# Ten weight splits by two transfers and scalar's negative, in the stage of the local attention

## The chip, the cores and the metric

The kernel runs on one core of a Trainium2 chip. The core has a matrix engine (TensorE, PE in the profile, with PEld for its weight loads), three engines for elementwise work (VectorE or DVE, ScalarE or ACT, GpSimd or POOL), a queue that only issues transfers (SyncE or SP), and 16 DMA engines that all queues share. Each engine works through its own queue strictly in order; a semaphore makes one wait for another. The metric is the device time of one execution in microseconds (us).

## The reference

One decoder layer on 512 tokens of width 1024, in float32. A shared normalised input h is multiplied by one wide matrix; its columns are split up for a recurrent branch, a local attention and their gates:

```python
h = rmsnorm(x, norm_mix_g[i])
proj = h @ w_in[i]
qk_ml, v_ml, o_ml, if_pre, q_sw, k_sw, v_sw, g_a, g_b = jnp.split(proj, split_idx, axis=-1)
qk_ml = jax.nn.silu(causal_depthwise_conv(qk_ml, conv_qk[i]))
...   # h_ml: chunkwise mLSTM of qk_ml, v_ml and gates, then y_a
y_b = swa_with_sinks(q_sw, k_sw, v_sw, sinks[i])   # 16 query heads, 4 key heads, window 128
merged = sigmoid(g_a) * (y_a @ w_branch_a[i]) + sigmoid(g_b) * (y_b @ w_branch_b[i])
x = x + merged @ w_out[i]
...   # squared-ReLU MLP of width 4096, a gated per-layer embedding, a last RMSNorm
```

What bears on the change: q_sw (1024 columns) and qk_ml (1024 columns) are each computed as eight projections of 128 columns, `w_qsw` and `w_qkml` in the kernel.

## The kernel before, in words

**Matmuls in three products.** TensorE multiplies in a rounded format (float32r). To keep float32's precision every operand is held as two tiles: a rounded part and the remainder that rounding left. A product is then three matmuls: rounded by rounded, rounded by remainder, remainder by rounded (`pairs`, `chain`, line 171). A projection (`proj_T`, `mm_T`) has 8 slices of the inner dimension, so 24 matmuls of 128x128 by 128x512.

**How a weight is split.** `load_w` takes a raw tile `wr` (128 x 1024 float32, 512 KB, four buffers) that a transfer from SP fills (`load_raw`, line 152). Then `split` makes the two parts: ACT casts it into `wh` (line 137), and DVE subtracts `wh` from `wr` into `wl` (line 138). `wh` and `wl` have four buffers each (`WB = 4`), shared by every weight of the kernel, so a weight can be split as soon as the weight four places earlier has been read by its last matmul.

**A split by transfer exists already.** `split_by_transfer` (lines 143 to 147) is used for eight sums of the activations: ACT casts the sum into the rounded part, ACT writes the sum's rounded negative into the second tile, and a transfer from POOL's queue adds the sum to that.

**The stage of the local attention.** Sixteen units of attention (`swa_probs`, `swa_out`; scores on PE at lines 689 and 690, copies and predicated copies at 700 and 701, exponentials on ACT at 712, the normalising product on DVE at 716, transposes at 726, the product with the values at 747, the split of the result into `yb` at 137 and 138) depend on long chains between PE, ACT and DVE. To keep PE at work beside them, eleven projections are put between the units as `fill`: `qk_proj(0)`, `q_proj(4)` to `q_proj(7)`, then `qk_proj` of 4, 1, 5, 2, 6 and 3. `qk_proj(7)` follows the loop. `q_proj` evicts its bank with a cast on ACT (424) and a subtraction on DVE (425); `qk_proj` with a scaled copy on ACT (666) and three multiply-adds on DVE (668), the convolution. Ahead of the stage stand the projections of the gates and `q_proj` 1 to 3; behind it the sigmoids of `silu` and the recurrent branch, with the eight projections of `w_b` between its steps.

**What sets the order.** The program's order gives priorities; when the program is built, a list scheduler walks through it with its own durations, and at each moment puts on every engine the ready instruction of highest priority. The result is one fixed order for each queue. Only the waits on semaphores are left for run time. So a change of one instruction can give other queues another order, too.

The parts that the change touches:

Of the kernel before, what the change touches and what calls it, by code (L numbers as in the profile page):

```python
# [11 lines left out]
F32R = mybir.dt.float32r  # L12
AF = mybir.ActivationFunctionType
ALU = mybir.AluOpType
AX = mybir.AxisListType

P = 128
# [3 lines left out]
KT = D // P  # L21
# [8 lines left out]
WB = 4  # L30
# [6 lines left out]
def block_kernel(  # L37
# [29 lines left out]
    nc = tc.nc  # L67
    V, A, G, T = nc.vector, nc.scalar, nc.gpsimd, nc.tensor


    def pool(stack, name, **kw):
        return stack.enter_context(tc.tile_pool(name=name, bufs=1, reuse_waits="tile", **kw))
# [4 lines left out]
    wp = pool(ctx, "wp")  # L77
# [9 lines left out]
    def nm(s):  # L87
        n_names[0] += 1
        return f"{s}_{n_names[0]}"


    def ps_g():
        return pp.tile([P, 512], F32, tag="g", bufs=2, name=nm("psg"))
# [12 lines left out]
    def act_f(n="f"):  # L106
        return ap.tile([P, 512], F32, tag="act", bufs=NACT, name=nm(n))

    def act_r(n="r"):
        return ap.tile([P, 512], F32R, tag="act", bufs=NACT, name=nm(n))  # L110
# [4 lines left out]
    def big_hl(n):  # L115

        hl = [bp.tile([P, KT, 512], F32R, tag="big", bufs=2, name=nm(n)) for _ in range(2)]
        return hl, [[t[:, k, :] for t in hl] for k in range(KT)]

    def tk(n):  # L120
        return tp_.tile([P, NH * (DV + 1)], F32, tag="tk", bufs=4, name=nm(n))
# [7 lines left out]
    def r32(t):  # L129
        return t.bitcast(F32)  # L130
# [3 lines left out]
    def split(dst, src, scale=None):  # L134

        if scale is None:
            A.copy(dst[0], src)  # L137
            last_low[0] = V.tensor_sub(dst[1], src, r32(dst[0]))  # L138
        else:
            A.activation(dst[0], src, AF.Copy, scale=scale)  # L140
            V.scalar_tensor_tensor(dst[1], src, scale, r32(dst[0]), ALU.mult, ALU.subtract)
# [8 lines left out]
    def load_raw(src, n):  # L150
        raw = wp.tile([P, 1024], F32, tag="wr", bufs=WRB, name=nm("wr"))
        nc.sync.dma_start(out=raw[:, :n], in_=src)
        return raw

    def load_w(src, n, dims, raw=None):

        if raw is None:
            raw = load_raw(src, n)
        parts = [wp.tile([P, 1024], F32R, tag=t, bufs=WB, name=nm(t))[:, :n] for t in ("wh", "wl")]
        split(parts, raw[:, :n])  # L160
        return [q.rearrange("p (k c) -> p k c", k=dims) for q in parts]

    def pairs(a, b):

        return [(a[0], b[0]), (a[0], b[1]), (a[1], b[0])]
# [3 lines left out]
    def chain(ps, ops, first, last, parts=False):  # L169
        for i, (l, r) in enumerate(ops):  # L170
            last_mm[0] = T.matmul(ps, l, r, start=first and i == 0, stop=last and i == len(ops) - 1, skip_group_check=parts)  # L171
# [13 lines left out]
    def mm_T(ps, w, acts, first=True, last=True):  # L185

        ops = []
        for k in range(len(acts)):
            ops += pairs([q[:, k, :] for q in w], acts[k])
        chain(ps, ops, first, last)  # L190
# [99 lines left out]
    h2, hT = big_hl("h")  # L290
# [49 lines left out]
    for m in range(NT):  # L340
# [7 lines left out]
        ps = ps_g()  # L348
        for c in range(3):
            mm_tok(ps[:, :264], wv[c], hT[K3[c]], m, first=c == 0, last=c == 2)  # L350
        t = sp.tile([P, 256], F32, tag="vs", bufs=4, name=nm("vs"))
# [1 line left out]
        gate_in = V.tensor_add(gt[:, m, :], ps[:, 256:264], bif)  # L353
        vs.append(t)

    def proj_T(wd, i, bank=ps_g):
        ps = bank()
        mm_T(ps, load_w(wd[i], KT * P, KT), hT)
        return ps

    dp = pool(ctx, "dp", space=bass.MemoryType.DRAM)
# [3 lines left out]
    with tc.issue_after(gate_in.ins):  # L365
        hi, lo = [r32(t[:, :, :P]) for t in h2]
# [37 lines left out]
    for i in range(2):  # L404
        ps = proj_T(w_ksw, i, ps_t)
        both = [act_r("kk"), act_r("kk")]
        low = [act_r("kl"), act_r("kl")]
        for ab in range(2):
            s, o = HALF[ab], HALF[1 - ab]
            A.copy(both[ab][s, :], ps[s, :])  # L410
            V.tensor_sub(low[ab][s, :], ps[s, :], r32(both[ab][s, :]))
            nc.sync.dma_start(out=r32(both[ab])[o, :], in_=r32(both[ab])[s, :])
            nc.sync.dma_start(out=r32(low[ab])[o, :], in_=r32(low[ab])[s, :])
        kk.append(both)
        kl.append(low)

    qs = {}

    def q_proj(i):
        ps = proj_T(w_qsw, i)  # L420
        for ab in range(2):
            s, o = HALF[ab], HALF[1 - ab]
            t = act_r("qs")
            A.copy(t[s, :], ps[s, :])
            V.tensor_sub(t[o, :], ps[s, :], r32(t[s, :]))
            qs[i, ab] = t

    q_proj(0)

    S3, S4 = [], []  # L430
# [48 lines left out]
    for m in range(NT):  # L479
        t = tk("vm").rearrange("p (h d) -> p h d", h=NH)  # L480
# [3 lines left out]
    def by_tokens(w, post, own_first=False):  # L484

        raws = quads(w, ["wr", "wr", "lm", "lm", "wr", "wr", "lm", "lm"])
        b = ps_a()
        X, Y, Z = [ps_t(), ps_t()], [b[:, :512], b[:, 512:]], [ps_g(), ps_g()]

        def prod(ps, f, w, kh, first, last=False):  # L490
            for t in range(2):
                ops = []
                for k in range(2):
                    ops += pairs([h[:, t * P : (t + 1) * P] for h in f[2 * kh + k]], [h[:, k, :] for h in w])
                chain(ps[t], ops, first and kh == 0, last and kh == 1, True)

        seven(lambda r: load_w(None, 1024, 2, r), prod, X, Y, Z, [raws[2 * i : 2 * i + 2] for i in range(4)], post, own_first)
# [70 lines left out]
    with tc.issue_after(last_mm[0].ins):  # L568
        for t in range(NT):
            for s in range(t + 1):  # L570
                c = (t * NT + s) * 4
                T.transpose(pgc[:, c : c + 4], gg[t][:, s * P : (s + 1) * P], ident[:4, :4])
            c = (NT * NT + t) * 4
# [22 lines left out]
    def gate_proj(wd):  # L596

        out_d = [None] * 4
        for j in range(2):
# [21 lines left out]
            def post(what, ps):  # L621
# [7 lines left out]
                else:  # L629
# [6 lines left out]
                    A.activation(o, ps, AF.Sigmoid)  # L636

            seven(lambda r: load_w(None, 1024, 4, r), prod, X, Y, Z, [raws[i : i + 1] for i in range(4)], post)
            for nh in range(2):
                d = dp.tile([P, 2, 512], F32, name=nm("gd"))  # L640
# [16 lines left out]
    for i in range(1, 4):  # L657
        q_proj(i)
# [1 line left out]

    qk = [None] * 8

    def qk_proj(i):
        ps = proj_T(w_qkml, i)
        acc = act_f("acc")
        A.activation(acc, ps, AF.Copy, scale=cw[:, i * 4 + 3 : i * 4 + 4])
        for s in range(1, 4):
            V.scalar_tensor_tensor(
                acc[:, s:], ps[:, : S - s], cw[:, i * 4 + 3 - s : i * 4 + 4 - s], acc[:, s:], ALU.mult, ALU.add
            )  # L670
        qk[i] = acc
# [86 lines left out]
    for n in (3, 2, 1):  # L758
        V.tensor_sub(vd[n], vs[n], vs[n - 1])

    fill = [lambda: qk_proj(0)] + [lambda i=i: q_proj(i) for i in range(4, 8)]
    fill += [lambda i=i: qk_proj(i) for i in (4, 1, 5, 2, 6, 3)]
    for u in range(LOOK):
        swa_probs(*units[u])
    for u in range(16):
# [4 lines left out]
        if u % 2:  # L770
            swa_out(*units[u][:2])

    qk_proj(7)

    for h in range(NH):
# [551 lines left out]
    for m in range(NT):  # L1327
        for o, n in ((0, 512),) if m == 0 else ((0, 256), (256, 256)):
            ps = ps_g()[:, :n]
# [108 lines left out]
```

## Time and profile before

| | |
|---|---|
| median of 3 runs | 880.56 us (880.06 to 881.1) |
| profiled execution | 879.82 us |
| its span, first to last instruction | 878.0 us |
| mean granted TensorE clock | 0.998 |
| PE busy | 866.8 us (99%) |
| DVE busy | 657.2 us (75%) |
| ACT busy | 483.5 us (55%) |
| POOL busy | 34.1 us (4%) |
| HBM read and written | 91.30 MB and 8.40 MB |

The profile is one execution. Its views: the page's totals; groups of instructions (line, engine, operation, out<-in by the program's names, count | busy us, mean ns | idle time ahead of them and who ended it); waits (who waited for whom: us, times, longest); the chain of waits that ended last, followed back from the end (start, us, what); timelines (start, us, instruction, idle ahead of it); and busy time by stage. Matmuls are pipelined and their ends are modelled, so one is drawn longer than the distance to the next. A line such as L137 can be a helper's, so the tile names tell more.

### The profile page before, as it was taken

How to read it: one execution, taken by the hardware profiler on the slowest of the kernel's cores; microseconds unless marked ns; L12 is line 12 of the kernel's file. 1: busy time of each engine (PE TensorE's matmuls, PEld its weight loads, DVE VectorE, ACT ScalarE, POOL GpSimd, SP SyncE). 2: the span in 40 equal slices, each digit the busy share in tenths (PEclk: the TensorE clock that was granted, in tenths of full speed). 3: DMA queues.
4: the chain of work that ended last, by engine and by line, in shares of the span. 5: the costliest groups of instructions: out<-in, count | busy, mean ns of one | idle time of the engine just before them, and what ended most of it. 6: DMA issues, size and time to landing. Idle time of an engine off the chain costs nothing.

```text
span 878.0 us, 11545 instructions
## 1 busy us (share of the span) xinstructions
PE 866.8 (99%) x4372; PEld 725.6 (83%) x4372; DVE 657.2 (75%) x966; ACT 483.5 (55%) x803; POOL 34.1 (4%) x58
## 2 busy tenths in 40 slices
PE   8999999999999999999999999999999999999996
PEld 7888889998777777788888888888888888888886
DVE  6999887875789876665896669756956794698557
ACT  6684554544676768743344665356435634564843
POOL 1111010000000000000020000000000000020000
PEclk9999999999999999999999999999999999999999
DMA  7765244435122162274244612530352054125302
GB/s 266 211 180 186 73 150 169 165 111 196 52 73 72 49 199 88 97 240 144 72 75 145 236 49 71 197 106 10 124 185 75 1 186 149 49 52 141 121 0 96
DMA packets 32793, 106.74 MB, mean 122 GB/s; under 512 B 4573, under 2 KB 4573, under 8 KB 32738
## 3 DMA queue, kind: packets, MB, share of 16 engines
q1 hardware_dynamic: 27570, 93.15, 31.2%
q0 software_dynamic: 5024, 12.59, 5.9%
q8 instruction: 34, 0.56, 0.3%
q10 hardware_dynamic: 144, 0.26, 0.1%
q14 instruction: 21, 0.17, 0.1%
HBM read 91.30 MB, written 8.40 MB: 114 GB/s over the span
## 4 chain that ended last, share of the span: by engine, by line
PE 90%; DVE 4%; ACT 3%; DMA 2%; issue 1%; SPq 0%; ACTq 0%; DVEq 0%
PE psg L171 50%; PE psp L171 23%; PE psa L171 7%; PE pst L171 4%; PE psa L831 1%; PE pst L747 1%; DVE wl L138 1%; DMA wr<-in_w_vsif 1%; ACT lm L712 1%; PE psa L819 1%; PE psa L689 1%; PE psa L690 1%; ACT wh L137 0%; DMA wr<-in_w_gb 0%; PE psp L980 0%
## 5 line engine op out<-in xcount | busy, mean ns | idle before, releaser
L137 ACT CAST wh<-wr 128x1024 fp32r<-128x1024 f32 x138 | 144.8, 1051 | 180.3 <-PE psg L171 74.8
L138 DVE TENSOR_TENSOR wl<-wr,wh 128x1024 fp32r<-128x1024 f32 x138 | 167.8, 1219 | 85.9 <-ACT wh L137 84.6
L171 PE MATMUL psg<-x,wh 128*128 128x512 f32 x512 | 157.7, 389 | 0.0
L171 PE MATMUL psp<-wh,uf 128*128 128x512 f32 x448 | 138.6, 389 | 0.0
L171 PEld LDWEIGHTS psg<-x,wh 128*128 128x128 f32 x512 | 96.0, 188 | 19.9
L171 PE MATMUL psg<-x,wl 128*128 128x512 f32 x256 | 99.6, 389 | 0.0
L171 PEld LDWEIGHTS psp<-wh,uf 128*128 128x128 f32 x448 | 84.1, 188 | 17.5
L171 PE MATMUL psp<-wl,uf 128*128 128x512 f32 x224 | 87.2, 389 | 0.0
L171 PE MATMUL psg<-h,wh 128*128 128x512 f32 x256 | 81.1, 395 | 0.7 <-DVE rc L715 0.7
L137 ACT CAST wh<-wd 128x1024 fp32r<-128x1024 f32 x44 | 46.2, 1052 | 54.0 <-PE psp L171 21.9
L138 DVE TENSOR_TENSOR wl<-wd,wh 128x1024 fp32r<-128x1024 f32 x44 | 53.1, 1217 | 14.7 <-ACT wh L137 14.5
L171 PEld LDWEIGHTS psg<-x,wl 128*128 128x128 f32 x256 | 48.0, 188 | 10.0
L171 PEld LDWEIGHTS psg<-h,wh 128*128 128x128 f32 x256 | 47.0, 188 | 11.2 <-issue 1.6
L171 PE MATMUL psg<-h,wl 128*128 128x512 f32 x128 | 50.5, 395 | 0.0
L138 DVE TENSOR_TENSOR uf<-F,uf 128x1792 fp32r<-128x1792 f32 (+2 forms) x20 | 33.0, 1652 | 21.8 <-ACT uf L137 21.8
L171 PEld LDWEIGHTS psp<-wl,uf 128*128 128x128 f32 x224 | 42.0, 188 | 8.7
L171 PE MATMUL psg<-yb,wh 128*128 128x512 f32 x128 | 41.3, 402 | 0.1
L171 PE MATMUL psg<-ya,wh 128*128 128x512 f32 x128 | 39.5, 390 | 0.0
L137 ACT CAST uf<-F 128x1792 fp32r<-128x1792 f32 (+2 forms) x20 | 27.9, 1396 | 20.5 <-DVE F L1133 20.4
L1157 DVE SCALAR_TENSOR_TENSOR xk<-psp,r,xk 128x512 f32<-128x512 f32 x48 | 33.7, 744 | 5.5 <-PE psp L171 5.2
L171 PE MATMUL psg<-hS,wh 128*128 128x256 f32 x192 | 35.6, 284 | 0.0
L171 PE MATMUL psa<-h,wh 128*128 128x256 f32 x192 | 35.3, 285 | 0.2 <-ACT p L625 0.2
(322 smaller groups left out, 1745.6 us busy)
## 6 DMA issues: line engine op xcount, KB each, us to landing
wr<-in_w_up SPq DMA_DIRECT2D x32, 512.0 KB, 3.3
wd<-in_w_down SPq DMA_DIRECT2D x24, 512.0 KB, 3.7
wr<-in_w_qsw SPq DMA_DIRECT2D x8, 512.0 KB, 4.3
gd<-gr POOLq DMA_DIRECT2D x8, 512.0 KB, 3.7
wr<-in_w_qkml SPq DMA_DIRECT2D x8, 512.0 KB, 3.2
wr<-in_w_b SPq DMA_DIRECT2D x8, 512.0 KB, 3.2
gl<-gd SPq DMA_DIRECT2D x8, 512.0 KB, 3.4
wr<-in_w_a SPq DMA_DIRECT2D x8, 512.0 KB, 4.4
```

The costliest lines, as they stand in the source:

```text
L137: A.copy(dst[0], src)
L138: last_low[0] = V.tensor_sub(dst[1], src, r32(dst[0]))
L171: last_mm[0] = T.matmul(ps, l, r, start=first and i == 0, stop=last and i == len(ops) - 1, skip_group_check=parts)
L689: T.matmul(o, q[:, n * P : (n + 1) * P], kk[kp][ab][:, k0 : k0 + 256], start=True, stop=False)
L690: T.matmul(o, q[:, n * P : (n + 1) * P], kl[kp][ab][:, k0 : k0 + 256], start=False, stop=True)
L712: A.activation(lm3[:, g, :], lm3[:, g, :], AF.Exp, bias=nmx[:, g : g + 1], scale=0.125, accum_out=sm[:, g : g + 1])
L747: T.matmul(o[HALF[ab], :], v[:, c : c + 64], w[:, ab * 512 : (ab + 1) * 512], start=j == 0, stop=j == len(terms) - 1)
L819: T.matmul(psc, qk[4 + h][:, n0 : n0 + P], qk[h][:, n0:], start=True, stop=True, skip_group_check=True)
L831: last_mm[0] = T.matmul(pn[:, t % 2, : DV + 1], wT[s][:, t * P : (t + 1) * P], vm[s][:, h, :], start=s == 0, stop=s == t, skip_group_check ...
L1157: V.scalar_tensor_tensor(o, ps[:, t, :], r2[:, 2 * toks + t : 2 * toks + t + 1], o, ALU.mult, ALU.add)
```

## The change

For the ten projections `q_proj(4)` to `q_proj(7)` and `qk_proj` of 4, 1, 5, 2, 6 and 3, the weight is no longer loaded raw by SP and split by ACT and DVE. A transfer from POOL's queue reads it from memory and casts it into `wh` on the way. ACT then writes the negative of `wh` into `wl`. A second transfer from POOL's queue reads the weight once more and adds it to `wl`, which leaves the remainder. The raw tile and DVE's subtraction go, ACT's cast becomes ACT's negative, and two transfers stand in place of one. `qk_proj(0)`, `qk_proj(7)` and every other weight stay as they were.

```diff
+    def load_by_dma(src, n, dims):
+        hi, lo = [wp.tile([P, 1024], F32R, tag=t, bufs=WB, name=nm(t))[:, :n] for t in ("wh", "wl")]
+        nc.gpsimd.dma_start(out=hi, in_=src)
+        A.activation(lo, r32(hi), AF.Copy, scale=-1.0)
+        nc.gpsimd.dma_start(out=lo, in_=src, accum_op=ALU.add)
+        return [q.rearrange("p (k c) -> p k c", k=dims) for q in (hi, lo)]
+
-    def load_w(src, n, dims, raw=None):
-
+    def load_w(src, n, dims, raw=None, by_dma=False):
+
+        if by_dma:
+            return load_by_dma(src, n, dims)
...
-    def proj_T(wd, i, bank=ps_g):
+    def proj_T(wd, i, bank=ps_g, by_dma=False):
         ps = bank()
-        mm_T(ps, load_w(wd[i], KT * P, KT), hT)
+        mm_T(ps, load_w(wd[i], KT * P, KT, by_dma=by_dma), hT)
...
-    fill = [lambda: qk_proj(0)] + [lambda i=i: q_proj(i) for i in range(4, 8)]
-    fill += [lambda i=i: qk_proj(i) for i in (4, 1, 5, 2, 6, 3)]
+    fill = [lambda: qk_proj(0)] + [lambda i=i: q_proj(i, True) for i in range(4, 8)]
+    fill += [lambda i=i: qk_proj(i, True) for i in (4, 1, 5, 2, 6, 3)]
```

`q_proj` and `qk_proj` take `by_dma=False` as well and hand it to `proj_T`.

More of the change, by code (lines that the diff above doesn't have):

```diff
@@ L417, in block_kernel, with q_proj @@
     qs = {}
-    def q_proj(i):
-        ps = proj_T(w_qsw, i)
+    def q_proj(i, by_dma=False):
+        ps = proj_T(w_qsw, i, by_dma=by_dma)
         for ab in range(2):
@@ L661, in block_kernel, with qk_proj @@
     qk = [None] * 8
-    def qk_proj(i):
-        ps = proj_T(w_qkml, i)
+    def qk_proj(i, by_dma=False):
+        ps = proj_T(w_qkml, i, by_dma=by_dma)
         acc = act_f("acc")
```

## The prediction

> **What bounds the kernel now.** I read the page first, for the engines' totals.
>
> ```profile
> PE 866.8 (99%) x4372; PEld 725.6 (83%) x4372; DVE 657.2 (75%) x966; ACT 483.5 (55%) x803; POOL 34.1 (4%) x58
> ```
>
> PE (TensorE) is busy for 866.8 of 878.0 us and the change takes no matmul away, so nothing that it does to another engine shows unless PE waits for that engine. The second view is the busy time by stage, for the stage that the change touches (from the first fill projection to the end of the local attention) and the one behind it.
>
> ```profile
> core 0: us, PE busy (x) PEld busy (x) DVE busy (x) ACT busy (x) POOL busy (x), PEclk, DMA share, GB/s
> 203.00:325.00 122.00, 120.72 (x616) 92.75 (x615) 94.11 (x199) 76.25 (x231) 0.88 (x2) 1.00 0.29 95
> 325.00:350.00 25.00, 24.87 (x108) 19.55 (x107) 18.38 (x36) 22.55 (x55) 0.00 (x0) 1.00 0.37 128
> ```
>
> In 122.00 us PE shows 1.28 us of idle time. DVE (VectorE) has 94.11 us of work there, ACT (ScalarE) 76.25, POOL (GpSimd) 0.88; the DMA engines are used to 0.29. So DVE is the busiest helper, but PE is the bound, and the gain can't be DVE's saving: it is at most what PE waits. The third view, the waits of PE in that window, names them all.
>
> ```profile
> PE psg L171 <- DVE rc L715: 0.7, 1, 0.7
> PE psa L689 <- DVE lm L701: 0.5, 1, 0.5
> PE pst L747 <- ACT pT L728: 0.2, 1, 0.2
> ```
>
> Idle time understates a wait, because each matmul is drawn longer than its pitch. The chain of waits gives the pitch (24 matmuls in 5.46 us, 0.2275 each; q1 to q3 run 72 of them without a gap) and the timeline of PE gives the starts around the two larger waits.
>
> ```profile
> 203.85 16.35 PE psg L171 x72
> 309.43 5.46 PE psg L171 x24
> ...
> 235.15 1.03 PE L726 MATMUL psa<-ident,lm 128*128 128x128 f32 x8
> 235.94 0.71 PE L171 MATMUL psg<-h,wh 128*128 128x512 f32 x2
> ...
> 263.00 0.39 PE L171 MATMUL psg<-h,wh 128*128 128x512 f32 x1
> 263.86 0.39 PE L689 MATMUL psa<-kk,qs 128*128 128x256 f32 x1 [0.47 <-DVE lm L701]
> ...
> 297.17 1.03 PE L726 MATMUL psa<-ident,lm 128*128 128x128 f32 x8
> 298.85 0.70 PE L171 MATMUL psg<-h,wh 128*128 128x512 f32 x2 [0.65 <-DVE rc L715]
> ```
>
> From 263.00 to 263.86 is 0.86 where 0.23 would do: a loss of 0.63. Eight transposes take 0.79 undisturbed (235.15 to 235.94) but 1.68 at 297.17: a loss of 0.89. These two are 1.52 us. Two smaller places remain:
>
> ```profile
> 239.03 0.39 PE L171 MATMUL psg<-h,wh 128*128 128x512 f32 x1
> 239.57 0.65 PE L747 MATMUL pst<-pT,vs 128*64 128x512 f32 x2 [0.16 <-ACT pT L728]
> ...
> 329.81 0.40 PE L171 MATMUL psg<-yb,wl 128*128 128x512 f32 x1
> 330.35 0.50 PE L171 MATMUL psg<-yb,wh 128*128 128x512 f32 x1
> ```
>
> Each is 0.54 where 0.23 would do, 0.31 lost, 0.62 together. So all that PE loses to others from 203 to 350 us is 2.14 us. That is the ceiling of this change.
>
> **The change part by part.** *DVE loses ten subtractions.* The groups of the window:
>
> ```profile
> L138 DVE TENSOR_TENSOR wl<-wr,wh 128x1024 fp32r<-128x1024 f32 x16 | 19.5, 1220 | 10.4 <-ACT wh L137 9.5 <-PE psg L171 0.8
> L137 ACT CAST wh<-wr 128x1024 fp32r<-128x1024 f32 x15 | 15.7, 1050 | 10.6 <-issue 6.8 <-PE psg L171 3.6 <-ACT yb L137 0.2
> ```
>
> Ten times 1.22 is 12.2 us of DVE's 94.11, and none of it is on PE's path by itself. Where it stands on the path is seen in the chain of waits ahead of the two larger losses:
>
> ```profile
> 242.61 0.16 ACT yb L137
> ...
> 254.42 1.23 DVE wl L138
> ...
> 296.41 0.69 ACT acc L666
> 297.22 0.17 DVE sm L713
> 297.39 1.31 DVE acc L668 x2
> ```
>
> The first loss, at 263.86, ends a chain that holds only DVE and ACT work from 242.61 us on, and the subtraction at 254.42 is a link of it. Without its 1.23 us the scores' matmul is free earlier by more than the 0.63 lost, so I count the 0.63 in full. The second loss is less sure: PE waits for a bank that DVE reads in L668, and these reads stand behind a sum (L713) that waits for ACT, which itself waits for PE until 296.41 (L666). The subtraction that goes, just before, shortens DVE's queue, but if the order of L713 and L668 stays, the 0.89 stays. I count half, 0.45. Sum: 1.08, say 1.1 us.
>
> *ACT trades ten casts for ten negatives.* No negative of 128x1024 stands in the trace. The rows of the sums that are split by transfer already have both kinds at half the size:
>
> ```profile
> L145 ACT CAST hS<-s x8: 603/607/622, 33.4 to 53.5; 128x512 fp32r<-128x512 f32 x8
> L146 ACT ACTIVATE hS<-s x8: 627/628/633, 33.9 to 54.0; 128x512 fp32r<-128x512 f32 x8
> L147 POOL DMA_DIRECT2D hS<-s x8: 837/852/1003, 34.8 to 54.9; - x8
> DMA to landing us min/median/max: 3.2/4.4/6.7
> ```
>
> 0.02 us more for 512 columns, so 0.02 to 0.04 each and at most 0.4 us over ten, on an engine with 45.75 us idle in the window: nothing, unless the place of the negative is bad (a rival below). It has a new wait, for the casting transfer, and behind it in ACT's queue stand the exponentials of the attention (L712), for which DVE and then PE wait.
>
> *POOL gets twenty transfers, SP loses ten.* An issue costs 0.53 us (a 512 KB store from POOL) to 0.85 (L147), so 10.6 to 17 us over ten weights on a queue that is empty: between its last store and the next transfer POOL has nothing.
>
> ```profile
> 205.69 0.53 POOL L641 DMA_DIRECT2D gd<-gr  x1 [2.35 <-ACT gr L636]
> 449.24 5.21 POOL L1033 DMA_DIRECT2D xk<-q  x6 [243.01 <-ACT q L1028]
> ...
> gd<-gr POOLq DMA_DIRECT2D x8, 512.0 KB, 3.7
> wr<-in_w_qkml SPq DMA_DIRECT2D x8, 512.0 KB, 3.2
> ```
>
> ```profile
> L152 SPq DMA_DIRECT2D wr<-in_w_qkml x8: 327/328/328, 194.6 to 255.7; - x8
> ```
>
> SP saves ten issues at 0.33 us, which nobody waits for; the loads of w_b behind them no longer wait for a free raw buffer and go out earlier, into the first casting transfers. The weights are read twice, 5 MB more in a stage where the DMA share is 0.29.
>
> *The new round trip.* A weight's two buffers come free when the projection four places earlier has read them, exactly as now. Then: issue, casting transfer, negative, issue, adding transfer, matmul. The tightest is the first (q4): its buffer is q1's, and q1 to q3 follow one another without attention work between them.
>
> ```profile
> 221.47 0.63 PE L171 MATMUL psg<-h,wh 128*128 128x512 f32 x2
> 325.23 0.63 PE L171 MATMUL psg<-yb,wh 128*128 128x512 f32 x2
> ...
> 209.18 1.05 ACT L137 CAST wh<-wr 128x1024 fp32r<-128x1024 f32 x1 [3.78 <-issue]
> ...
> 228.73 0.63 PE L171 MATMUL psg<-h,wh 128*128 128x512 f32 x2
> ```
>
> The first two rows are the first matmul of the twelve projections from qk0 to qk7 and the first one behind them. The cast shows when the buffer was free, the matmul when the weight is needed: 19.55 us of lead. No casting transfer is in the trace; the nearest rows are 3.7 us (the POOL store of the same size) and 3.2 (the SP load). I take 3.7, with ends at 3.2 and 7.4, twice that. The adding transfer has 256 KB in 4.4 us; for 512 KB the ends are 4.4 and 8.8, and I take the middle, 6.6. The trip is 0.85 + 3.7 + 1.05 + 0.85 + 6.6 = 13.05, at the far ends 0.85 + 7.4 + 1.05 + 0.85 + 8.8 = 18.95, and some wait in ACT's queue on top. POOL's own rhythm (issue, landing, negative, issue) is 0.85 + 3.7 + 1.05 + 0.85 = 6.45 us per weight, below the 8.6 us at which the stage uses them on average (221.47 to 325.23 for twelve projections). So PE does not wait for the transfers: cost 0, and if the cover were gone, the trip's excess over 19.55, once.
>
> Does DVE's work hold up POOL's issues? The eight issues of L147 took 0.837 to 1.003 us, with DVE at work beside them. The Trainium skill, "SBUF — State Buffer", section "Who interferes with whom", speaks against moving loads to this queue: GpSimd and VectorE share a port pair, and a VectorE copy, cast or tensor-scalar in a two-port mode locks out GpSimd, which then can't write descriptors. The groups of DVE in this window hold no copy, cast or tensor-scalar, so by that rule too the issues stay short and the sum is the same; were one blocked behind a DVE instruction, the trip would be about 1.2 us longer, inside the lead, and only the late negative below would become likelier.
>
> **Sum.** The profiled execution took 879.82 us, 1.82 over its span and 0.74 under the median of 880.56. 879.82 - 1.1 = 878.7 for such a run, and against the median 880.56 - 1.1 = 879.5. That is 0.12%, below the 0.2% that I treat as the least a measurement of this kernel can tell from no change.
>
> **The rivals.** *All of PE's waits go.* The order of the queues is drawn anew at build time, with a DVE that is 12.2 us lighter; if no loss of the 2.14 us is left and none is new, 878.4, faster by 0.24%. For it: every loss but the last lies in this window, and DVE is the busiest helper. Against: two of the four end on ACT's work, which doesn't shrink.
>
> *Nothing goes.* The 0.89 and the small ones hang on ACT, and new waits take the place of the 0.63: 880.6.
>
> *The negative comes too early in ACT's queue* (slower). The order is fixed at build time by a guess of when the casting transfer lands; if it lands later by d, ACT stands at the negative for d and the attention's exponentials behind it are late by d. DVE's freed 1.22 us make up for that much, so it decides from d = 1.2 on. Landings of 512 KB differ by more than this between queues and times:
>
> ```profile
> DMA to landing us min/median/max: 3.0/3.3/7.4
> ```
>
> (the raw loads of all the weights, by line). With d = 2 at all ten, 7.8 us; about half of the ten lie where the chain is DVE and ACT work and PE has no lead, so 3.9: 884.5. For it: the chain from 242.61 to 263.86 has no slack at all. Against: ACT is idle for 45.75 of 122 us, mostly waiting for others, and the landing of most loads is close to 3.3.
>
> *The adding transfer is late for PE* (slower). At the far ends and behind 3 us in ACT's queue the first trip is 22 us, 2.4 over the lead, and PE waits 2.4 at 228.73: 880.56 - 1.1 + 2.4 = 881.9; if it holds for the second weight too, 884.3. Against: the middle of the estimates leaves 6 us.
>
> **How the numbers follow.** The forecast has 0.33; nothing goes 0.11; all waits go 0.18; the late negative 0.30; the late adding transfer 0.08. Faster is the third, 0.18; within 0.2% the first two, 0.44; slower the last two, 0.38. The likeliest case's own range is 878.8 to 880.6 (both larger losses gone, or none). The range over all runs from 878.3 (the ceiling) to 884.6 (the priced late negative and the late second transfer); what is left out is a worse late negative.
>
> **What would show it.** Right: POOL with some 15 us more work from 209 us on, DVE's work in the stage near 82 us, ten L138 rows of wl fewer, no PE wait for L701 near 263, casting transfers that land in about 4 us, adding ones in 5 to 9. The late negative: ACT's waits led by a DMA into wh, and exponentials behind it; PE's waits on scores or transposes over 3 us. The late transfer: a PE wait on a DMA into wl at the first of the ten. I am wrong if PE's busy total moves (its work is the same), or if the stage changes by more than 2.1 us downwards.

## The result, and the profile after

The changed kernel takes 885.55 us (median of five, 885.26 to 886.13) against 880.17 us before: ratio 1.0061, 95% interval 1.0048 to 1.0074. It is slower by 5.4 us. The forecast was 879.5, with a range up to 884.6; the direction of the likeliest case was wrong, and the time lies outside the range.

The page's totals after (lines of the changed file stand ten below those of before from L171 on, so `chain` is L181 and the scores L699 and L700):

```profile
PE 869.2 (98%) x4372; PEld 727.3 (82%) x4372; DVE 647.1 (73%) x956; ACT 484.5 (55%) x803; POOL 48.1 (5%) x78
```

DVE lost ten instructions and 10.1 us (12.2 were worked out), POOL gained twenty and 14.0 us (10.6 to 17). PE's own total, which was not to move, rose by 2.4 us, of which the slow clock shown below makes about 1.7. The busy time by stage says where the loss is (start and end, busy us of PE, PEld, DVE, ACT and POOL, granted clock, DMA share):

```profile
203.00:220.00 17.00, 17.00 (x81) 14.21 (x80) 5.10 (x7) 4.96 (x7) 3.03 (x5) 1.00 0.69 199
220.00:240.00 20.00, 17.86 (x90) 15.00 (x88) 9.45 (x21) 10.76 (x28) 3.08 (x5) 0.91 0.53 127
240.00:265.00 25.00, 23.14 (x113) 17.07 (x114) 18.18 (x46) 18.70 (x60) 4.20 (x7) 1.00 0.56 127
```

PE is idle for 2.14 us of the stretch from 220 to 240 us, and of the whole stage in that stretch alone its granted clock is below 1.00, at 0.91. PE's waits after and ACT's longest ones:

```profile
PE psa L699 <- DVE qs L435: 2.0, 1, 2.0
...
PE pst L757 <- ACT pT L738: 0.9, 2, 0.6
PE psa L736 <- DVE lm L711: 0.8, 1, 0.8
PE psa L699 <- DVE lm L711: 0.7, 1, 0.7
PE psg L181 <- DVE acc L678: 0.5, 1, 0.5
...
ACT wl L159 <- DMA wh<-in_w_qsw: 13.7, 4, 5.7
ACT wl L159 <- DMA wh<-in_w_qkml: 8.5, 6, 1.9
```

ACT now stands for 22.2 us at the ten negatives (L159), waiting for the casting transfers. The timelines of ACT, DVE and PE (start, us, instruction, idle ahead of it) show how the longest wait of PE comes about:

```profile
216.31 0.58 ACT L434 CAST qs<-psg 64x512 fp32r<-64x512 f32 x1 [0.75 <-DVE qs L435]
221.61 1.06 ACT L159 ACTIVATE wl<-wh 128x1024 fp32r<-128x1024 f32 x1 [4.72 <-DMA wh<-in_w_qsw]
222.69 0.58 ACT L434 CAST qs<-psg 64x512 fp32r<-64x512 f32 x1
...
223.30 0.68 DVE L435 TENSOR_TENSOR qs<-psg,qs 64x512 fp32r<-64x512 f32 x1 [5.68 <-ACT qs L434]
...
221.65 0.39 PE L181 MATMUL psg<-h,wh 128*128 128x512 f32 x1
224.04 0.53 PE L699 MATMUL psa<-kk,qs 128*128 128x256 f32 x1 [1.99 <-DVE qs L435]
...
225.01 0.63 PE L181 MATMUL psg<-h,wl 128*128 128x512 f32 x1
225.44 1.05 PE L181 MATMUL psg<-h,wh 128*128 128x512 f32 x2
226.29 0.63 PE L181 MATMUL psg<-h,wl 128*128 128x512 f32 x1
...
227.56 0.28 PE L699 MATMUL psa<-kk,qs 128*128 128x256 f32 x1
```

ACT waits 4.72 us at the negative of q5. Behind it stands the eviction of q3 (L434), behind that DVE's half of it (L435), and behind that the scores of the first attention unit. From 221.65 to 224.04 PE does one matmul: 2.39 us for 0.23, a loss of 2.16. Then comes what no part of the prediction had: from 225.01 to 225.44 one matmul takes 0.43 us, nearly twice the pitch of 0.2275, and so on to 227.56. The two score matmuls and seven of 128x512 from 224.04 to 227.56 took 3.52 us; by the pitches of before (0.12 and 0.2275) they need 1.83. The slow clock costs 1.69 us, and the first wait with it 3.85 us, about seven tenths of the whole loss. The rest is the smaller waits, from 240 to 293 us.

Why the negative waits is read from POOL's own queue:

```profile
209.86 0.53 POOL L158 DMA_DIRECT2D wh<-in_w_qsw  x1 [3.46 <-PE psg L181]
214.96 0.87 POOL L160 DMA_DIRECT2D wl<-in_w_qsw  x1 [4.56 <-ACT wl L159]
215.52 0.87 POOL L158 DMA_DIRECT2D wh<-in_w_qsw  x1
222.96 0.85 POOL L160 DMA_DIRECT2D wl<-in_w_qsw  x1 [6.57 <-ACT wl L159]
223.51 0.84 POOL L158 DMA_DIRECT2D wh<-in_w_qsw  x1
...
DMA to landing us min/median/max: 3.6/5.9/6.7
DMA to landing us min/median/max: 5.3/5.5/5.5
```

(the last two lines: landings of the casting transfers, L158, and of the adding ones, L160). The first casting transfer goes out alone at 209.86 and the negative runs at 213.60. The second can't go out when its buffer is free, since in POOL's queue it stands behind the first adding transfer, which waits for the first negative; it goes out 0.56 us behind that transfer, and the negative that needs it starts 6.1 us later. Five of the ten casting transfers are issued so, about 0.55 us behind an adding one, and a sixth 1.4 us behind: these six land in 5.8 to 6.7 us. The other four, issued alone or more than 3 us after an adding one, land in 3.6 to 4.7. The packets in the trace show what the landing waits for: the 128 packets of the first adding transfer start from 216.55 to 219.63 us (0.33 us each), and the 128 of the casting transfer issued 0.56 us later only from 219.70 to 221.09 us (0.17 us each). The two don't run side by side; the second stands behind the first.

### The profile page after: what moved, and what is told of

Read it like the earlier page. It is cut to its first block, busy times and chain, and to the rows that moved or that the text cites. A ratio compares the mean times of both kernels' runs of the same rounds, so it can differ in the third digit from the quotient of the medians.

```text
span 884.0 us, 11548 instructions
## 1 busy us (share of the span) xinstructions
PE 869.2 (98%) x4372; PEld 727.3 (82%) x4372; DVE 647.1 (73%) x956; ACT 484.5 (55%) x803; POOL 48.1 (5%) x78
## 4 chain that ended last, share of the span: by engine, by line
PE 69%; issue 4%; ACT 2%; DVE 2%; DMA 1%; POOL 1%; POOLq 0%; ACTq 0%
PE psg L181 39%; PE psp L181 23%; PE psa L841 1%; PE pst L757 1%; DMA wh<-in_w_qkml 1%; PE psa L181 1%; PE psa L829 1%; ACT lm L722 1%; POOL wh L158 0%; PE psp L990 0%; PE psa L736 0%; PE pst L883 0%; PE psp L998 0%; ACT dm L812 0%; POOL wl L160 0%
## 5 line engine op out<-in xcount | busy, mean ns | idle before, releaser
L137 ACT CAST wh<-wr 128x1024 fp32r<-128x1024 f32 x128 | 134.3, 1051 | 171.8 <-PE psg L181 71.7
L138 DVE TENSOR_TENSOR wl<-wr,wh 128x1024 fp32r<-128x1024 f32 x128 | 155.6, 1220 | 75.0 <-ACT wh L137 74.7
L181 PE MATMUL psg<-x,wh 128*128 128x512 f32 x512 | 157.8, 389 | 0.0
L181 PE MATMUL psp<-wh,uf 128*128 128x512 f32 x448 | 138.6, 389 | 0.0
L181 PEld LDWEIGHTS psg<-x,wh 128*128 128x128 f32 x512 | 96.0, 188 | 19.9
L181 PE MATMUL psg<-x,wl 128*128 128x512 f32 x256 | 99.6, 389 | 0.0
L181 PEld LDWEIGHTS psp<-wh,uf 128*128 128x128 f32 x448 | 84.1, 188 | 17.5
L181 PE MATMUL psp<-wl,uf 128*128 128x512 f32 x224 | 87.2, 389 | 0.0
L181 PE MATMUL psg<-h,wh 128*128 128x512 f32 x256 | 81.8, 399 | 0.5 <-DVE acc L678 0.5
L181 PEld LDWEIGHTS psg<-h,wh 128*128 128x128 f32 x256 | 47.7, 191 | 11.3 <-issue 1.6
L181 PEld LDWEIGHTS psg<-x,wl 128*128 128x128 f32 x256 | 48.0, 188 | 10.0
L181 PE MATMUL psg<-h,wl 128*128 128x512 f32 x128 | 51.1, 400 | 0.0
L181 PEld LDWEIGHTS psp<-wl,uf 128*128 128x128 f32 x224 | 42.0, 188 | 8.7
L181 PE MATMUL psg<-yb,wh 128*128 128x512 f32 x128 | 41.2, 400 | 0.0
L181 PE MATMUL psg<-ya,wh 128*128 128x512 f32 x128 | 39.5, 390 | 0.0
L181 PE MATMUL psa<-h,wh 128*128 128x256 f32 x192 | 35.3, 285 | 0.3 <-ACT p L635 0.3
L181 PE MATMUL psg<-hS,wh 128*128 128x256 f32 x192 | 35.6, 284 | 0.0
```

## The experiments

Theory A: ACT stands at the negative because the casting transfer lands late, and what is behind it in ACT's queue reaches PE late. Theory B: the transfers themselves cost, by reading the weights twice beside the attention. Theory C: the order drawn anew is worse by itself.

**The negative on GpSimd.**

```diff
-        A.activation(lo, r32(hi), AF.Copy, scale=-1.0)
+        G.tensor_scalar_mul(lo, r32(hi), -1.0)
```

> The ten negatives are made by GpSimd instead of ScalarE; both transfers stay. Theory A (ScalarE stands at the negative until the casting transfer lands, 22.1 us of waits, and the attention's work behind it comes late): ScalarE has no such wait, the wait for q3's scores at 224 us and the half clock behind it go, 879 to 880.5 us. Theory B (the transfers themselves cost: the weights are read twice, 20 transfers beside the attention): they are all still there, so 884 to 886 us. Theory C (the order drawn anew at build time is worse by itself): between, 882 to 885.

Measured: 886.79 us, ratio 1.0067 (1.0054 to 1.0079). No theory had it this slow. ACT's waits for transfers are gone, and so is the wait at 224 us, but another has come (waits of PE; timelines of POOL and PE):

```profile
PE psg L181 <- DMA wl<-in_w_qkml: 5.9, 3, 2.9
...
218.60 0.91 POOL L160 DMA_DIRECT2D wl<-in_w_qsw  x1 [0.30 <-POOL wl L159]
219.22 0.87 POOL L158 DMA_DIRECT2D wh<-in_w_qsw  x1
225.93 2.77 POOL L159 TENSOR_SCALAR wl<-wh 128x1024 fp32r<-128x1024 f32 x1 [5.84 <-DMA wh<-in_w_qsw]
229.00 0.90 POOL L160 DMA_DIRECT2D wl<-in_w_qsw  x1 [0.30 <-POOL wl L159]
...
305.79 0.50 PE L181 MATMUL psg<-h,wl 128*128 128x512 f32 x1 [2.93 <-DMA wl<-in_w_qkml]
...
306.69 0.63 PE L181 MATMUL psg<-h,wl 128*128 128x512 f32 x1
307.12 1.05 PE L181 MATMUL psg<-h,wh 128*128 128x512 f32 x2
```

From one adding transfer to the next are 10.4 us (218.60 to 229.00), more than the 8.6 at which PE uses the weights, so the last remainders are late. The run doesn't decide between A and B by its time. It shows the prediction's late adding transfer, brought about here by a slower round trip, and again the slow pitch behind a wait of 2.93 us. Behind the second longest of its waits, 1.76 us at 265 us, the clock stays at 1.00.

**The casting transfer alone.**

```diff
+        raw = load_raw(src, n)
         nc.gpsimd.dma_start(out=hi, in_=src)
-        A.activation(lo, r32(hi), AF.Copy, scale=-1.0)
-        nc.gpsimd.dma_start(out=lo, in_=src, accum_op=ALU.add)
+        V.tensor_sub(lo, raw[:, :n], r32(hi))
```

> The casting transfer stays; the raw weight is loaded by SP as before and VectorE subtracts, so negative and adding transfer go. ScalarE loses ten casts (10.5 us), VectorE is as before. Theory A: no wait of ScalarE for a landing; with no adding transfer ahead of it each casting transfer lands in 3.6 to 3.9 us; VectorE may wait for it at a few subtractions. 879.5 to 881.5 us. Theory B: half of the loss stays, since the weights are still read twice: 882 to 884.

Measured: 879.23 us, ratio 0.9987 (0.9978 to 0.9996). The weights are read twice here too, and nothing is lost: against B, as far as the casting transfers and the second reading go. Casting transfers land in 3.4 to 4.9 us, median 4.0, and DVE waits for them twice, 3.7 us in total, without PE coming late.

**One negative later.** q5's negative is queued behind q3's second eviction (`behind[0]` holds that one):

```diff
-        A.activation(lo, r32(hi), AF.Copy, scale=-1.0)
+        with tc.issue_after(behind[0]) if behind[0] is not None else ExitStack():
+            A.activation(lo, r32(hi), AF.Copy, scale=-1.0)
...
```

> As changed, but q5's negative alone is queued behind q3's second eviction on ScalarE. Theory A: the wait of 2.0 us for q3's scores and the stretch of half clock behind it go (about 2.2 + 1.7 us), the smaller waits from 238 us on stay: 881 to 882.5 us. Theory B: 885 to 886, since no transfer changes.

Measured: 882.86 us, ratio 1.0028 (1.0019 to 1.0037). Half of the loss goes by moving one instruction in one queue, with every transfer still made. The wait at q3's scores is gone and the clock from 220 to 240 us is 1.00. It is less than the 3.85 us that stood there, because ACT still waits 15.3 us for casting transfers and the later waits of PE have grown (1.6 us at transposes, 1.3 at the product with the values).

**Without the adding transfers.** The remainders hold only the negatives.

```diff
-        nc.gpsimd.dma_start(out=lo, in_=src, accum_op=ALU.add)
```

> The ten adding transfers are left out, so the ten remainders hold only the negative and the products are those of other numbers. Theory A with its cause in the queue (a casting transfer issued 0.55 us behind an adding one shares the DMA engines with it): all casting transfers land in 3.6 to 3.9 us instead of a median of 5.9, ScalarE waits 5 to 10 us instead of 22, 880 to 882 us. If casting is slow by itself, the landing stays near 6 us and the time near 885.

Measured: 879.9 us, ratio 0.9996 (0.9987 to 1.0005). The landings of the casting transfers:

```profile
DMA to landing us min/median/max: 3.4/3.5/5.0
```

Median 3.5 us instead of 5.9: casting isn't slow by itself, and the adding transfer ahead of it is what it waits for. ACT's waits at the negatives fall to 11.9 us, somewhat more than expected, and the time is back at that of before.

**All negatives later.** Each negative is queued behind the last eviction, on ACT, of the projection three places earlier:

```diff
-        A.activation(lo, r32(hi), AF.Copy, scale=-1.0)
+        with tc.issue_after(evictions[-3]):
+            A.activation(lo, r32(hi), AF.Copy, scale=-1.0)
...
```

> As changed, but each negative is queued on ScalarE behind the last eviction of the projection three places earlier, one projection after its buffers came free. Theory A: ScalarE's 22.1 us of waits for casting transfers fall below 5, the waits of PE in the stage fall to 1 to 2 us, 879 to 880.5 us. If the 20 transfers or the new order cost something by themselves, 882 us or more remain.

Measured: 879.24 us against 880.3, ratio 0.9989 (0.998 to 0.9998). Both transfers, the negatives on ACT and VectorE's saving are as in the changed kernel; only the places in ACT's queue are set otherwise, and with them POOL's and the other queues' orders are drawn anew. The stage, POOL's queue and the landings of the casting and the adding transfers:

```profile
220.00:240.00 20.00, 19.92 (x107) 16.53 (x107) 13.11 (x29) 13.89 (x39) 3.35 (x5) 1.00 0.70 159
240.00:265.00 25.00, 24.93 (x135) 19.46 (x132) 18.97 (x46) 19.71 (x60) 4.20 (x6) 1.00 0.59 127
...
280.00:300.00 20.00, 20.00 (x111) 16.34 (x110) 15.68 (x37) 16.11 (x47) 2.28 (x3) 1.00 0.37 80
...
215.82 0.53 POOL L160 DMA_DIRECT2D wh<-in_w_qsw  x1 [4.62 <-PE psg L184]
219.09 0.87 POOL L163 DMA_DIRECT2D wl<-in_w_qsw  x1 [2.73 <-ACT wl L162]
221.26 0.54 POOL L160 DMA_DIRECT2D wh<-in_w_qsw  x1 [1.30 <-PE psg L184]
...
DMA to landing us min/median/max: 3.4/3.7/4.6
DMA to landing us min/median/max: 5.2/5.5/8.4
```

The casting transfer now waits for its buffer (PE) and not for the adding one, lands in 3.7 us (median), and ACT has no wait for a transfer left. PE is idle for 0.08 and 0.07 us in two stretches that had lost 2.14 and 1.86. The loss goes by the places of the negatives, with all twenty transfers made and an order drawn anew as well. This settles A, and speaks against B and C.

**The cast one weight ahead, the negative on GpSimd.** As in the first experiment, but each casting transfer is issued before the negative of the weight ahead of it:

```diff
+        hi = casting.pop(0) if casting else cast_in(src, n)
+        if coming:
+            casting.append(cast_in(coming.pop(0), n))
...
+        with tc.issue_after(last_cast[0]):
+            G.tensor_scalar_mul(lo, r32(hi), -1.0)
+            nc.gpsimd.dma_start(out=lo, in_=src, accum_op=ALU.add)
```

> The negative on GpSimd again, but each casting transfer is issued ahead of the negative of the weight before it, so that its landing runs beside that. GpSimd's rhythm was 10.3 us per weight (0.9 + 6.4 + 2.8 + 0.3), above PE's 8.6; now it is 0.9 + 2.8 + 0.9 plus what is left of the wait, 5 to 7. Theory A with GpSimd's rhythm as the new wait: no PE wait for a remainder, 878.5 to 880 us. If GpSimd's negatives slow VectorE, 881 to 883.

Measured: 879.95 us, ratio 0.9998 (0.9989 to 1.0007). The late remainders are gone, as is POOL's wait for castings (0.3 us left), so POOL's rhythm was the cause in the first experiment. One wait of 1.3 us for DVE remains in the stage.

**A wait on purpose.** What set the half clock was open: the length of PE's wait, or the transfers beside it. In the kernel before, without any of the change's transfers, idle copies on ACT hold up q3's evictions, and PE keeps its order:

```diff
+        if i == 2:
+            for _ in range(9):
+                with tc.issue_after(held[0]):
+                    held[0] = A.activation(act_f("idle"), r32(h2[0])[:, 0, :], AF.Copy).ins
...
```

> The kernel before, with nine idle copies of 128x512 on ScalarE ahead of q3's evictions and PE held to its old order behind the scores that need them; no transfer changes. If a wait of PE of about 2 us makes the granted clock fall for some us after it, then matmuls at twice the pitch follow, and the time rises by the wait and 1.5 to 2 us more: 883.5 to 885. If the half clock in the changed kernel came from the transfers, the time rises by the wait alone: 882 to 882.5.

> As the stall on purpose, with ten idle copies in place of nine. The wait of 1.66 us at q3's scores left the pitch of the matmuls at 0.23 us; the changed kernel's wait of 1.99 us was followed by 0.43. With ten copies the wait is about 2.2 us. If the length of the wait decides, matmuls at about 0.43 follow for some 3.5 us and the time rises by 0.5 and 1.5 us over nine copies (885.3); if something else in the changed kernel set the clock (the transfers), the pitch stays 0.23 and the time is 883.8.

> Thirteen idle copies: a wait of about 3.7 us. If the length of the wait decides, the half clock follows in any case, for at least as long as in the changed kernel: 887 us or more. If the transfers set it: 885.4.

Measured: 883.31 us with nine copies, 885.68 with ten (four runs, 884.32 to 886.75), 886.98 with thirteen (two runs): 3.0, 5.8 and 7.1 us above the kernel before, timed beside each. Timelines of PE with nine and with ten:

```profile
224.81 0.39 PE L701 MATMUL psa<-kk,qs 128*128 128x256 f32 x1 [1.66 <-DVE qs L430]
...
225.39 0.62 PE L173 MATMUL psg<-h,wh 128*128 128x512 f32 x2
225.84 0.39 PE L173 MATMUL psg<-h,wl 128*128 128x512 f32 x1
```

```profile
225.01 0.42 PE L701 MATMUL psa<-kk,qs 128*128 128x256 f32 x1 [2.18 <-DVE qs L430]
...
225.87 1.05 PE L173 MATMUL psg<-h,wh 128*128 128x512 f32 x2
226.72 0.63 PE L173 MATMUL psg<-h,wl 128*128 128x512 f32 x1
...
239.76 1.09 PE L740 MATMUL psa<-ident,lm 128*128 128x128 f32 x8 [0.72 <-DVE lm L715]
241.64 0.50 PE L173 MATMUL psg<-h,wh 128*128 128x512 f32 x1 [0.78 <-DVE acc L679]
```

After 1.66 us of idle time two matmuls take 0.45, after 2.18 us 0.85. So a wait alone brings the half clock; no transfer of the change is needed. The run with nine copies came out between its two expectations, with no half clock but with another wait of 0.8 us in the stage.

The length of one wait is not the whole rule, though. Here are the slow stretch of the changed kernel with the time just ahead of it, and the two slow stretches with ten copies (start and end, length, busy us of PE, PEld, DVE, ACT and POOL, granted clock, DMA share):

```profile
220.70:224.12 3.42, 1.43 (x12) 1.11 (x10) 0.68 (x1) 1.74 (x3) 1.16 (x2) 1.00 0.11 37
224.12:227.54 3.42, 3.42 (x9) 2.78 (x10) 2.07 (x3) 0.48 (x1) 0.23 (x1) 0.50 0.89 144
...
225.23:228.64 3.41, 3.41 (x10) 2.74 (x10) 2.60 (x3) 0.56 (x1) 0.00 (x0) 0.50 0.34 124
242.30:245.71 3.41, 3.41 (x9) 1.53 (x6) 3.32 (x8) 2.12 (x9) 0.00 (x0) 0.50 0.10 13
```

Each lasts 3.41 us. The second one with ten copies follows no long wait, only the two of 0.72 and 0.78 us shown above; the run with nine copies has the same two waits, at 238.00 and 239.88 us, and its clock stays at 1.00 there. With thirteen copies the wait is 3.73 us, and the slow stretch begins only 1.4 us after its end, at 228.51. So the length of one wait doesn't decide alone; what else does stays open. The second slow stretch fits the 2.4 us between nine and ten copies, more than the 2 us expected. It is seen in the one execution profiled, the slowest of four.

## Why the prediction was wrong, point by point

**Right.** DVE's 81.17 us in the stage (foretold near 82), POOL's 15.08 us there against 0.88 before (some 15 more were foretold), the reading twice for nothing, and the tightest round trip: in the changed kernel no matmul waits for a remainder. The adding transfer, taken at 6.6 us, takes 5.5. No run gains more than the ceiling of 2.14 us.

**The sum of 1.1 us** is met in its number: with the negatives in a place where they wait for nothing, the gain is 880.3 - 879.24 = 1.06 us (0.2 to 1.8 by the interval). That is in part luck, for there PE waits for no engine any more in the stage, where the sum had counted half of the second loss. Nor is VectorE's relief shown to be what brings it: the run with the casting transfer alone leaves VectorE its subtractions, takes ScalarE's ten casts away and gains 0.99 us, and the run with the cast one weight ahead takes the subtractions away too and gains 0.35. The 0.63 counted in full depends on the order, too: the wait of the scores for VectorE's predicated copy is still there in the changed kernel (0.7 us, L699 for L711), and is 1.3 us with the cast one weight ahead.

**The step that failed** is "nothing, unless the place of the negative is bad". It was bad, and the sign of the result hangs on it. ACT's waits at the ten negatives, put at nothing, are 22.2 us, and the one of 4.72 us makes PE late by 2.16 us. The rival was there, with its sign, its mechanism and the queue behind it, at 0.30 against 0.33 for the forecast. What kept it below was a casting transfer of 3.7 us for each weight. That is what one takes alone. The prediction wrote POOL's rhythm as issue, landing, negative, issue, one weight after the other, 6.45 us, and so had itself put each casting transfer right behind an adding one; it did not ask how long the second stands behind the first on the DMA engines. Measured from one adding transfer to the next are 8.0 us (214.96 to 222.96), with 6.1 for the casting transfer in place of 3.7.

**The price** of the rival, 3.9 us, was too low, so that the range ended at 884.6. Its d of 2 us was close (22.2 us over ten weights), and the waits without the clock come to 5.4 - 1.7 = 3.7 us. The 1.69 us of half clock were not in any term: every wait of PE was counted at its length. Without them the time would be 883.9, inside the range. The Trainium skill, "TensorE: Matmul & The Clock Gate", section "Part 1: The HAM clock gate (the "warmup" mystery)", tells of a clock that goes to half after an idle window of about 3.4 us, free-running. The traces agree in the half (0.43 against 0.2275 us), and the slow stretches last 3.41 us; they differ in the idle time that brings them, for waits of 1.99 and 2.18 us were enough, and PE shows 1.43 us of work in the 3.42 us ahead of the slow stretch.

**The second loss** (0.89 us at 297 us, counted half): it is gone in the run with all negatives later, 20.00 of 20.00 us busy from 280 to 300, so there it could have been counted in full. It is gone with the casting transfer alone as well (20.00 too), where VectorE keeps its work, so it doesn't hang on that work alone.

**POOL's issues** took 0.53 to 0.87 us in the stage, as foretold. The window does hold predicated copies by VectorE (L701), which the prediction's "no copy" passes over, and the issues stayed short beside them.

## What to carry to other kernels

When work moves from an engine to a transfer, the new wait stands in an in-order queue, and its place there decides more than the work saved: here one place was worth +5.4 us and another -1.1. Two transfers that depend on each other through an engine should not follow one another directly in one queue, since the second kind holds up the next of the first kind and then stands ahead of it on the DMA engines; let a transfer wait for its buffer alone. A wait of a busy TensorE can cost more than its length: from 1.99 us on, every wait seen here had a slow stretch behind it, worth about 1.7 us.

## What the runs showed of the hardware

- Behind waits of TensorE of 1.99, 2.18, 2.93 and 3.73 us the granted clock was 0.50 for 3.41 us, with matmuls at 0.43 us instead of 0.2275; that costs about 1.7 us. Behind single waits of 1.66 and 1.76 us it stayed at 1.00, but in the stage it fell once behind two of 0.72 and 0.78 us close together.
- A 512 KB casting transfer landed in 3.5 us (median of the run without adding transfers, 3.4 to 5.0), and in 5.8 to 6.7 issued within 1.4 us of an adding one of the same size, whose packets start first (seen in the pair above). The adding one took 5.3 to 5.5 us there, with single ones up to 8.4 in another run.
- GpSimd negates 128x1024 float32 in 2.77 us, where ScalarE takes 1.06.
